# High and low parts of the transposed activations, interleaved token by token

## The chip, the cores and the metric

The kernel runs on one core of a Trainium2 chip. The metric is the device time of one execution in microseconds. All times of the profile come from one profiled execution, counted from the start of its span.

## The reference

One decoder layer on 256 tokens of width 4096: an RMS norm, one wide projection, two token mixers (chunked gated linear attention, GLA, and sliding-window attention with sinks, SWA), a gated merge, an output projection, a residual and a final norm.

```python
h = rms_norm(x, norm_gains[l])
z = h @ w_in[l]                       # 4096 -> 19472 columns
(gq, gk, gv, gg, gdec, sq, sk, sv, sg, ga, gb) = split_columns(z, IN_SPLITS)
...
o_a = gla_mix(gq, gk, gv, log_a)      # per-head norm and a SiLU gate follow
y_a = (o_a * silu(gg)) @ w_gla_out[l]
o_b = swa_sink_mix(sq, sk, sv, sinks[l])
y_b = (o_b * silu(sg)) @ w_swa_out[l]
merged = sigmoid(ga + b_gates[l, 0]) * y_a + sigmoid(gb + b_gates[l, 1]) * y_b
x = x + merged @ w_out[l]
return rms_norm(x, final_norm_gain)
```

(Shapes and casts are left out.) Everything is fp32.

## The kernel before

Nearly all of the work is in `gemm` (line 125), which multiplies 256 tokens by a block of 512 weight columns. Both operands are split into a high part, a copy rounded to the type F32R, and a low part, the difference. A product is then the sum of three matmuls, which lines 136 to 138 issue for each k tile of 128 rows and each of the two token tiles of 128: high times high, high times low, low times high. In them the activations are the stationary operand (the weights of the array, in TensorE's sense: 128 x 128, taken by a weight load before each matmul), and the weight matrix of the layer is the moving one, 128 x 512. They add up in one PSUM tile `acc` for each token tile.

The weight matrices stream from memory two k tiles at a time (`raw`, line 148, on SP's queue). ScalarE makes their high part (line 154), VectorE their low part (line 155), into staging tiles of three buffers. The scheduler orders by data and by priority; the loads and splits are raised by `tc.high_priority`.

The activations lie transposed in SBUF, 128 values of the k dimension on the partitions and tokens along the row. There are four such tiles: `hT` (the input times its gain, 32 k tiles; its first contents are made in `first_inputs` by ScalarE on line 107 and VectorE on line 108 during the first block, gq 0), `oaT` and `obT` (the outputs of the two mixers, 16 k tiles each) and `mT` (the merged output, 32 k tiles, in the place of `hT`). The last three are written by `transpose_split` (line 177): TensorE transposes into PSUM (line 184), and `split_to` makes the high part on ScalarE (line 174) and the low part on VectorE (line 175), two k tiles at a time. Of `mT`, seven of the eight groups are issued together, in the last step of the merge loop, and the eighth in the first block of the output projection.

In each of these tiles the layout is [partition, k tile, high or low, token], so that a weight load on lines 136 to 138 reads 128 neighbouring values.

Besides `gemm`, one more place reads `hT`: the low-rank input of the decays (line 215) uses it as the moving operand, 512 columns of both parts, with 32 columns of weights, into the PSUM tile `dps`; lines 219 and 220 add the two halves of the result into `gd`.

The order of the stages is: gq 0, gk 0, the decays, then for two groups of heads gq, gk, gv, gg with the GLA mixer in between; sk, sv; the eight blocks of the GLA output projection (`ya`); sq and sg four times with the SWA mixer; then ga, gb and the SWA output projection (`yb`) eight times; and the eight blocks of the output projection (`o`).

Of the kernel before, what the change touches and what calls it, by code (L numbers as in the profile page):

```python
# [8 lines left out]
F32 = mybir.dt.float32  # L9
F32R = mybir.dt.float32r  # L10
AF = mybir.ActivationFunctionType
ALU = mybir.AluOpType
AX = mybir.AxisListType

P = 128
S = 256
# [3 lines left out]
KT = DM // P  # L20
KW = 2
GH, DK, DV = 8, 128, 256
RANK = 16
CH = 64
HQ, HKV, HD = 32, 8, 64
OKT = 2048 // P
# [4 lines left out]

# 512-column blocks of w_in, in the order in which the host lays them out.
BLOCKS = []
# [13 lines left out]
def trunk_kernel(  # L47
# [18 lines left out]
    nc = tc.nc  # L66
# [20 lines left out]
    def rms_scale(o, ssum, n):  # L87
        """o = (ssum / n + eps) ** -0.5"""
        nc.vector.tensor_scalar(o, ssum, 1.0 / n, EPS, ALU.mult, ALU.add)
        nc.gpsimd.tensor_tensor(o, o, mhalf[:, : o.shape[1]], ALU.pow)  # L90

# [1 line left out]
    hT = big.tile([P, KT, 2, S], F32R, tag="hT", name="hT")  # L93

    xsb = big.tile([P, KT, S], F32, tag="oT", name="xsb")

    def first_inputs(gp, ssq):
        """Loads the input as the first block needs it; its squares add up in ssq."""

        def before(k0, n):  # L100
            with tc.high_priority(PRIO):
                if k0 < 4 or k0 % 4 == 0:
                    m = n if k0 < 4 else 4
                    nc.sync.dma_start(xsb[:, k0 : k0 + m, :], xT[:, k0 : k0 + m, :])
                for kt in range(k0, k0 + n):
                    g = gin_sb[:, kt : kt + 1]
                    nc.scalar.activation(hT[:, kt, 0, :], xsb[:, kt, :], AF.Copy, scale=g)
                    nc.vector.scalar_tensor_tensor(
                        hT[:, kt, 1, :], xsb[:, kt, :], g, hT[:, kt, 0, :].bitcast(F32), ALU.mult, ALU.subtract
                    )  # L110
            xr = xsb[:, k0 : k0 + n, :]
            if k0 < KW:
                nc.scalar.activation(ssq[:, k0 : k0 + n, :], xr, AF.Square)
                return
            sq = gp.tile([P, KW, S], F32, tag="sq", name=f"sq{k0}", bufs=2)
            nc.scalar.activation(sq, xr, AF.Square)
            nc.gpsimd.tensor_tensor(ssq, ssq, sq, ALU.add)

        return before
# [5 lines left out]
    def gemm(name, lhs, w, nkt, before=None, chunks=WHOLE, trail=0, hold=None):  # L125
        """Both token tiles of lhs.T @ w for one block of 512 columns. The second tile's products
        with the last `trail` chunks come after all of the first tile's; those of these chunks
        that the staging area can't keep until then are in `hold`."""
        acc = [acc_ps.tile([P, NB], F32, tag="acc", name=f"{name}_a{t}") for t in range(NT)]

        def products(t, k0, n, hi, lo):
            ts = slice(t * P, (t + 1) * P)
            for i in range(n):
                kt = k0 + i
                lh, ll = lhs[:, kt, 0, ts], lhs[:, kt, 1, ts]
                nc.tensor.matmul(acc[t], lh, hi[:, i, :], start=kt == 0, stop=False)  # L136
                nc.tensor.matmul(acc[t], lh, lo[:, i, :], start=False, stop=False)  # L137
                nc.tensor.matmul(acc[t], ll, hi[:, i, :], start=False, stop=kt == nkt - 1)  # L138

        chunks = [c for c in chunks if c[0] < nkt]  # L140
        held = []
        for ci, (k0, n) in enumerate(chunks):
            left = len(chunks) - ci
            if before is not None:
                before(k0, n)
            with tc.high_priority(PRIO):
                raw = stage.tile([P, n, NB], F32, tag="raw", name=f"{name}_r{k0}", bufs=4)
                nc.sync.dma_start(raw, w[k0 // KW][:, k0 % KW : k0 % KW + n, :])
                if STG < left <= trail:
                    hi, lo = hold[:, trail - left, 0], hold[:, trail - left, 1]  # L150
                else:
                    hi = stage.tile([P, n, NB], F32R, tag="hi", name=f"{name}_h{k0}")
                    lo = stage.tile([P, n, NB], F32R, tag="lo", name=f"{name}_l{k0}")
                nc.scalar.copy(hi, raw)  # L154
                nc.vector.tensor_tensor(lo, raw, hi.bitcast(F32), ALU.subtract)  # L155
            products(0, k0, n, hi, lo)
            if left <= trail:
                held.append((k0, n, hi, lo))
            else:
                products(1, k0, n, hi, lo)  # L160
        for h in held:
            products(1, *h)
        return acc
# [7 lines left out]
    def split_to(dst, src_ps):  # L171
        """dst[:, ..hi/lo.., :] from a PSUM tile of the same layout less the hi/lo axis."""
        hi, lo = dst
        nc.scalar.copy(hi, src_ps)
        nc.vector.tensor_tensor(lo, src_ps, hi.bitcast(F32), ALU.subtract)

    def transpose_split(oT, kt0, src, nk, name):
        """src [tokens, t, nk*128] -> oT[:, kt0:kt0+nk, hi/lo, tokens]"""
        for k2 in range(0, nk, 2):
            tp = pst(f"{name}_t{k2}")  # L180
            for k in range(2):
                for t in range(NT):
                    c = (k2 + k) * P
                    nc.tensor.transpose(
                        tp[:, k * S + t * P : k * S + (t + 1) * P], src[:, t, c : c + P], ident
                    )
            v = tp.rearrange("p (k s) -> p k s", k=2)
            ks = slice(kt0 + k2, kt0 + k2 + 2)
            split_to((oT[:, ks, 0, :], oT[:, ks, 1, :]), v)

    # ================= gated linear attention =================
    with tc.tile_pool(name="gla", bufs=1) as gp:
        ssq = gp.tile([P, KW, S], F32, name="ssq")
        q0 = zblock("gq", 0, before=first_inputs(gp, ssq), chunks=RAMP)
        k0 = zblock("gk", 0)
        oaT = big.tile([P, OKT, 2, S], F32R, tag="oT", name="oaT")

        # per-token scale of the input norm
        xps = pst("xps")
# [6 lines left out]

        # low-rank decay input, transposed: rows 0-15 from w's high part, 16-31 from its low part
        wd_raw = stage.tile([P, KT, RANK], F32, tag="raw", name="wd_raw", bufs=4)
# [5 lines left out]
        for kt in range(KT):  # L214
            nc.tensor.matmul(
                dps[0 : 2 * RANK, :], wd[:, kt], hT[:, kt], start=kt == 0, stop=kt == KT - 1
            )
        gd = gp.tile([2 * RANK, S], F32, name="gd")
        nc.scalar.copy(gd, dps[0 : 2 * RANK, 0:S])
        nc.vector.tensor_tensor(gd, gd, dps[0 : 2 * RANK, S : 2 * S], ALU.add)  # L220
        rps = pst("rps")
# [17 lines left out]
        def headsT(name, acc, scale):  # L239
            """[tokens, 4 heads x 128] in PSUM -> [128, head, token]"""  # L240
            zt = gp.tile([P, NT, NB], F32, tag="zt", name=f"{name}_z")
# [19 lines left out]
        for g in range(2):  # L261
            accq = q0 if g == 0 else zblock("gq", g)
            qT = headsT(f"gq{g}", accq, DK**-0.5)

            # log decays of the group's heads and their running sums in each chunk
            l = gp.tile([P, 4, S], F32, tag="e0", name=f"l{g}")
# [49 lines left out]
            nc.vector.tensor_tensor(kT, kT, d, ALU.mult)  # L316
            # keys of chunks 0 and 1 as chunks 2 and 3 see them
            k2 = gp.tile([P, 4, 2 * CH], F32, tag="k2", name=f"k2{g}")
# [7 lines left out]
            for p in range(2):  # L326
# [5 lines left out]

                # o = A @ v, a head at a time; A is kept transposed, [key, query]
                accg = None
# [55 lines left out]

    # ================= sliding-window attention =================
    late = ctx.enter_context(tc.tile_pool(name="late", bufs=1))
    ya = late.tile([P, NT, DM], F32, tag="ya", name="ya")
    with tc.tile_pool(name="swa", bufs=1) as sp:
# [37 lines left out]

        obT = big.tile([P, OKT, 2, S], F32R, tag="oT", name="obT")
        for i in range(4):
# [62 lines left out]

    # ================= gates and merge =================
    def merged(n):
        transpose_split(mT, n * 4, ya[:, :, n * NB : (n + 1) * NB], 4, f"m{n}")  # L500

    with tc.tile_pool(name="mrg", bufs=1) as mp:
        for n in range(NBLK):
# [11 lines left out]
            if n == NBLK - 1:  # L515
                mT = big.tile([P, KT, 2, S], F32R, tag="hT", name="mT")
                for m in range(n):
                    merged(m)
# [6 lines left out]

    # ================= output projection, residual, final norm =================
    with tc.tile_pool(name="fin", bufs=1) as fp:
# [38 lines left out]
def _tiles(w, nblk):  # L566
    """[K, nblk*512] -> [block, K group, partition, k tile, 512], contiguous for each load."""
    import numpy as np

    k = w.shape[0]  # L570
    w = w.reshape(k // (KW * P), KW, P, nblk, NB)
    return np.ascontiguousarray(w.transpose(3, 0, 2, 1, 4))
# [55 lines left out]
```

## Time and profile before

| | us |
|---|---|
| median of 3 runs (lowest to highest) | 2496.63 (2496.22 to 2498.13) |
| span of the profiled execution | 2494.7 |
| TensorE busy (PE) | 2469.9 (99%) |
| weight loads busy (PEld) | 2033.3 (82%) |
| VectorE busy (DVE) | 1306.1 (52%) |
| ScalarE busy (ACT) | 1093.1 (44%) |
| GpSimd busy (POOL) | 41.4 (2%) |

The profile counts TensorE's matmuls (PE) and its weight loads (PEld) as two engines. Matmuls are pipelined and their ends are modelled, so a matmul's shown time is longer than the step from one start to the next; the starts are what tells the pace. The time of the profiled execution is its span, 2494.7 us; the time of a run holds some 2 us more.

### The profile page before, as it was taken

How to read it: one execution, taken by the hardware profiler on the slowest of the kernel's cores; microseconds unless marked ns; L12 is line 12 of the kernel's file. 1: busy time of each engine (PE TensorE's matmuls, PEld its weight loads, DVE VectorE, ACT ScalarE, POOL GpSimd, SP SyncE). 2: the span in 40 equal slices, each digit the busy share in tenths (PEclk: the TensorE clock that was granted, in tenths of full speed). 3: DMA queues.
4: the chain of work that ended last, by engine and by line, in shares of the span. 5: the costliest groups of instructions: out<-in, count | busy, mean ns of one | idle time of the engine just before them, and what ended most of it. 6: DMA issues, size and time to landing. Idle time of an engine off the chain costs nothing.

```text
span 2494.7 us, 28744 instructions
## 1 busy us (share of the span) xinstructions
PE 2469.9 (99%) x11220; PEld 2033.3 (82%) x11220; DVE 1306.1 (52%) x1303; ACT 1093.1 (44%) x1289; POOL 41.4 (2%) x52
## 2 busy tenths in 40 slices
PE   8999999999999999999999999999999999999998
PEld 6788888888888888888888888888888888888886
DVE  8565555545444455555555454555545456544544
ACT  6444444434444444544444444444444444444443
POOL 4000000000000000000000000000000000000000
PEclk9999999999999999999999999999999999999999
DMA  7455555445555545454465556665666555665655
GB/s 258 156 175 188 170 175 195 175 168 188 194 192 195 193 148 193 150 171 166 150 211 199 198 198 197 197 202 197 198 196 198 194 194 177 236 211 203 211 203 186
DMA packets 132985, 474.32 MB, mean 190 GB/s; under 512 B 15056, under 2 KB 15440, under 8 KB 132720
## 3 DMA queue, kind: packets, MB, share of 16 engines
q1 hardware_dynamic: 127584, 461.69, 54.5%
q10 hardware_dynamic: 5264, 10.79, 1.4%
q8 instruction: 88, 1.44, 0.2%
q14 instruction: 49, 0.40, 0.0%
HBM read 468.23 MB, written 4.19 MB: 189 GB/s over the span
## 4 chain that ended last, share of the span: by engine, by line
PE 95%; DVE 2%; issue 1%; ACT 1%; DMA 0%; POOL 0%; SPq 0%; ACTq 0%; POOLq 0%; DVEq 0%
PE ga_a L137 5%; PE ga_a L136 5%; PE gb_a L137 5%; PE gb_a L136 5%; PE ga_a L138 5%; PE gb_a L138 5%; PE o_a L136 5%; PE o_a L137 5%; PE o_a L138 5%; PE sg_a L137 2%; PE sg_a L136 2%; PE sg_a L138 2%; PE sq_a L138 2%; PE sq_a L137 2%; PE ya_a L136 2%; PE ya_a L137 2%
## 5 line engine op out<-in xcount | busy, mean ns | idle before, releaser
L155 DVE TENSOR_TENSOR ga_l<-ga_r,ga_h 128x1024 fp32r<-128x1024 f32 x128 | 156.8, 1225 | 171.6 <-ACT ga_h L154 171.6
L155 DVE TENSOR_TENSOR gb_l<-gb_r,gb_h 128x1024 fp32r<-128x1024 f32 x128 | 156.9, 1225 | 171.1 <-ACT gb_h L154 171.1
L155 DVE TENSOR_TENSOR o_l<-o_r,o_h 128x1024 fp32r<-128x1024 f32 x124 | 152.0, 1225 | 161.4 <-ACT o_h L154 161.3
L154 ACT CAST ga_h<-ga_r 128x1024 fp32r<-128x1024 f32 x128 | 135.2, 1057 | 209.8 <-PE ga_a L138 171.5
L154 ACT CAST gb_h<-gb_r 128x1024 fp32r<-128x1024 f32 x128 | 135.2, 1056 | 204.5 <-PE gb_a L138 159.4
L154 ACT CAST o_h<-o_r 128x1024 fp32r<-128x1024 f32 x124 | 131.0, 1056 | 193.2 <-PE o_a L138 186.2
L138 PE MATMUL ga_a<-ga_h,hT 128*128 128x512 f32 x512 | 199.4, 389 | 0.0
L137 PE MATMUL ga_a<-ga_l,hT 128*128 128x512 f32 x512 | 199.2, 389 | 0.0
L136 PE MATMUL ga_a<-ga_h,hT 128*128 128x512 f32 x512 | 199.2, 389 | 0.0
L138 PE MATMUL gb_a<-gb_h,hT 128*128 128x512 f32 x512 | 199.2, 389 | 0.0
L136 PE MATMUL gb_a<-gb_h,hT 128*128 128x512 f32 x512 | 199.2, 389 | 0.0
L137 PE MATMUL gb_a<-gb_l,hT 128*128 128x512 f32 x512 | 199.2, 389 | 0.0
L138 PE MATMUL o_a<-o_h,mT 128*128 128x512 f32 x496 | 193.0, 389 | 0.0
L137 PE MATMUL o_a<-o_l,mT 128*128 128x512 f32 x496 | 193.0, 389 | 0.0
L136 PE MATMUL o_a<-o_h,mT 128*128 128x512 f32 x496 | 192.9, 389 | 0.0
L155 DVE TENSOR_TENSOR ya_l<-ya_r,ya_h 128x1024 fp32r<-128x1024 f32 x64 | 78.4, 1226 | 95.6 <-ACT ya_h L154 95.6
L155 DVE TENSOR_TENSOR sq_l<-sq_r,sq_h 128x1024 fp32r<-128x1024 f32 x64 | 78.4, 1225 | 84.8 <-ACT sq_h L154 84.8
L155 DVE TENSOR_TENSOR yb_l<-yb_r,yb_h 128x1024 fp32r<-128x1024 f32 x64 | 78.4, 1225 | 82.8 <-ACT yb_h L154 82.8
L155 DVE TENSOR_TENSOR gg_l<-gg_r,gg_h 128x1024 fp32r<-128x1024 f32 x64 | 78.3, 1224 | 75.9 <-ACT gg_h L154 75.9
L155 DVE TENSOR_TENSOR sg_l<-sg_r,sg_h 128x1024 fp32r<-128x1024 f32 x64 | 78.3, 1223 | 72.7 <-ACT sg_h L154 72.7
L154 ACT CAST sg_h<-sg_r 128x1024 fp32r<-128x1024 f32 x64 | 67.4, 1053 | 111.0 <-PE sg_a L138 94.7
L155 DVE TENSOR_TENSOR gv_l<-gv_r,gv_h 128x1024 fp32r<-128x1024 f32 x64 | 78.2, 1224 | 67.9 <-ACT gv_h L154 67.9
(278 smaller groups left out, 5568.3 us busy)
## 6 DMA issues: line engine op xcount, KB each, us to landing
ga_r<-in_win_dram SPq DMA_DIRECT2D x128, 512.0 KB, 4.3
gb_r<-in_win_dram SPq DMA_DIRECT2D x128, 512.0 KB, 4.2
o_r<-in_wout_dram SPq DMA_DIRECT2D x128, 512.0 KB, 3.3
gv_r<-in_win_dram SPq DMA_DIRECT2D x64, 512.0 KB, 3.2
gg_r<-in_win_dram SPq DMA_DIRECT2D x64, 512.0 KB, 3.3
ya_r<-in_wgla_dram SPq DMA_DIRECT2D x64, 512.0 KB, 3.2
sq_r<-in_win_dram SPq DMA_DIRECT2D x64, 512.0 KB, 3.2
sg_r<-in_win_dram SPq DMA_DIRECT2D x64, 512.0 KB, 3.3
```

The costliest lines, as they stand in the source:

```text
L136: nc.tensor.matmul(acc[t], lh, hi[:, i, :], start=kt == 0, stop=False)
L137: nc.tensor.matmul(acc[t], lh, lo[:, i, :], start=False, stop=False)
L138: nc.tensor.matmul(acc[t], ll, hi[:, i, :], start=False, stop=kt == nkt - 1)
L154: nc.scalar.copy(hi, raw)
L155: nc.vector.tensor_tensor(lo, raw, hi.bitcast(F32), ALU.subtract)
```

## The change

In `hT`, `oaT`, `obT` and `mT` the two innermost axes change places: the layout becomes [partition, k tile, token, high or low]. The high and the low value of a token are neighbours, and a weight load reads 128 values with one value between each two. All writers and readers of these tiles follow. For the decays, the moving operand is still the same 512 neighbouring values, and the two halves of the result, which now alternate too, are picked out of PSUM with a step. (The diff also takes out comments and docstrings, which is not shown.)

```diff
-    hT = big.tile([P, KT, 2, S], F32R, tag="hT", name="hT")
+    hT = big.tile([P, KT, S, 2], F32R, tag="hT", name="hT")
...
-                    nc.scalar.activation(hT[:, kt, 0, :], xsb[:, kt, :], AF.Copy, scale=g)
+                    nc.scalar.activation(hT[:, kt, :, 0], xsb[:, kt, :], AF.Copy, scale=g)
                     nc.vector.scalar_tensor_tensor(
-                        hT[:, kt, 1, :], xsb[:, kt, :], g, hT[:, kt, 0, :].bitcast(F32), ALU.mult, ALU.subtract
+                        hT[:, kt, :, 1], xsb[:, kt, :], g, hT[:, kt, :, 0].bitcast(F32), ALU.mult, ALU.subtract
                     )
...
-                lh, ll = lhs[:, kt, 0, ts], lhs[:, kt, 1, ts]
+                lh, ll = lhs[:, kt, ts, 0], lhs[:, kt, ts, 1]
...
-            split_to((oT[:, ks, 0, :], oT[:, ks, 1, :]), v)
+            split_to((oT[:, ks, :, 0], oT[:, ks, :, 1]), v)
...
-        oaT = big.tile([P, OKT, 2, S], F32R, tag="oT", name="oaT")
+        oaT = big.tile([P, OKT, S, 2], F32R, tag="oT", name="oaT")
...
-                dps[0 : 2 * RANK, :], wd[:, kt], hT[:, kt], start=kt == 0, stop=kt == KT - 1
+                dps[0 : 2 * RANK, :], wd[:, kt], hT[:, kt].rearrange("p s h -> p (s h)"), start=kt == 0, stop=kt == KT - 1
...
-        nc.scalar.copy(gd, dps[0 : 2 * RANK, 0:S])
-        nc.vector.tensor_tensor(gd, gd, dps[0 : 2 * RANK, S : 2 * S], ALU.add)
+        d2 = dps[0 : 2 * RANK, :].rearrange("p (s h) -> p h s", h=2)
+        nc.scalar.copy(gd, d2[:, 0, :])
+        nc.vector.tensor_tensor(gd, gd, d2[:, 1, :], ALU.add)
...
-        obT = big.tile([P, OKT, 2, S], F32R, tag="oT", name="obT")
+        obT = big.tile([P, OKT, S, 2], F32R, tag="oT", name="obT")
...
-                mT = big.tile([P, KT, 2, S], F32R, tag="hT", name="mT")
+                mT = big.tile([P, KT, S, 2], F32R, tag="hT", name="mT")
```

## Rows read from the trace of the kernel before

**Rows 1.** The page: busy us (share) and instructions by engine; granted clock by slice.

```profile
PE 2469.9 (99%) x11220; PEld 2033.3 (82%) x11220; DVE 1306.1 (52%) x1303; ACT 1093.1 (44%) x1289; POOL 41.4 (2%) x52
...
PEclk9999999999999999999999999999999999999999
```

**Rows 2.** The page: the chain that ended last, by engine.

```profile
PE 95%; DVE 2%; issue 1%; ACT 1%; DMA 0%; POOL 0%; SPq 0%; ACTq 0%; POOLq 0%; DVEq 0%
```

**Rows 3.** The timeline (start us, us, engine, line) inside a ga block.

```profile
1500.19 0.39 PE L137 MATMUL ga_a<-ga_l,hT 128*128 128x512 f32 x1
1500.20 0.19 PEld L138 LDWEIGHTS ga_a<-ga_h,hT 128*128 128x128 f32 x1
1500.42 0.39 PE L138 MATMUL ga_a<-ga_h,hT 128*128 128x512 f32 x1
...
1503.82 0.39 PE L138 MATMUL ga_a<-ga_h,hT 128*128 128x512 f32 x1
```

**Rows 4.** Weight loads by shape: count | busy us, mean ns | idle before.

```profile
L138 PEld LDWEIGHTS ga_a<-ga_h,hT 128*128 128x128 f32 x512 | 96.1, 188 | 19.9
...
L215 PEld LDWEIGHTS dps<-hT,wd 128*32 128x32 f32 x32 | 3.4, 109 | 3.7
L345 PEld LDWEIGHTS at<-qs,ks 128*64 128x64 f32 x32 | 3.1, 134 | 0.0
```

**Rows 5.** Tile dps: duration ns min/median/max, first and last start us.

```profile
L215 PE MATMUL dps<-hT,wd x32: 387/392/400, 102.9 to 110.0; 128*32 128x512 f32 x32
```

**Rows 6.** Timeline in the SWA mixer: loads of 128 columns for matmuls of 64.

```profile
910.27 0.30 PEld L481 LDWEIGHTS so<-sv,pT 128*128 128x128 f32 x2 [0.21 <-ACT pT L480]
...
910.49 0.30 PEld L482 LDWEIGHTS so<-sv,pT 128*128 128x128 f32 x2
```

**Rows 7.** Timeline in the first block, after a wait of TensorE for data.

```profile
26.27 0.19 PEld L137 LDWEIGHTS gq_a<-gq_l,hT 128*128 128x128 f32 x1 [0.32 <-DVE gq_l L155]
26.27 0.50 PE L137 MATMUL gq_a<-gq_l,hT 128*128 128x512 f32 x1
...
26.38 0.19 PEld L138 LDWEIGHTS gq_a<-gq_h,hT 128*128 128x128 f32 x1
26.61 0.40 PE L138 MATMUL gq_a<-gq_h,hT 128*128 128x512 f32 x1
```

**Rows 8.** VectorE's groups by shape: a copy with a step, one without.

```profile
L308 DVE COPY dec<-e 128x16 f32<-128x16 f32 x2 | 0.3, 170 | 0.0
...
L224 DVE COPY rb<-rstd 128x32 f32<-128x32 f32 x2 | 0.3, 178 | 0.8 <-POOL rstd L90 0.8
```

**Rows 9.** TensorE's matmuls by shape: the slowest and an undisturbed group.

```profile
L137 PE MATMUL ga_a<-ga_l,hT 128*128 128x512 f32 x512 | 199.2, 389 | 0.0
...
L137 PE MATMUL gq_a<-gq_l,hT 128*128 128x512 f32 x128 | 51.4, 402 | 5.2 <-DVE gq_l L155 5.2
```

**Rows 10.** First 60 us: busy of PE, PEld, DVE, ACT, POOL; low halves; first matmul.

```profile
0.00:60.00 60.00, 49.07 (x199) 37.80 (x200) 49.44 (x52) 42.61 (x71) 26.22 (x25) 1.00 0.75 262
...
L108 DVE SCALAR_TENSOR_TENSOR hT<-xsb,gin_sb,hT 128x256 fp32r<-128x256 f32 x32 | 27.1, 897 | 4.4 <-ACT hT L107 4.4
...
3.81 0.48 DVE L108 SCALAR_TENSOR_TENSOR hT<-xsb,gin_sb,hT 128x256 fp32r<-128x256 f32 x1 [3.81 <-ACT hT L107]
...
5.39 0.80 PE L136 MATMUL gq_a<-gq_h,hT 128*128 128x512 f32 x1 [5.39 <-ACT gq_h L154]
```

**Rows 11.** The splits by shape, VectorE's and ScalarE's.

```profile
L155 DVE TENSOR_TENSOR ga_l<-ga_r,ga_h 128x1024 fp32r<-128x1024 f32 x128 | 156.8, 1225 | 171.6 <-ACT ga_h L154 171.6
...
L175 DVE TENSOR_TENSOR mT<-m_t,mT 128x512 fp32r<-128x512 f32 x16 | 9.9, 682 | 0.3 <-ACT mT L174 0.3
...
L154 ACT CAST ya_h<-ya_r 128x1024 fp32r<-128x1024 f32 x64 | 67.6, 1057 | 95.3 <-PE ya_a L138 91.3 <-PE sv_a L138 4.0
...
L174 ACT CAST mT<-m_t 128x512 fp32r<-128x512 f32 x16 | 8.7, 591 | 0.3
```

**Rows 12.** Busy by engine around the transposes of mT.

```profile
2100.00:2130.00 30.00, 29.96 (x161) 25.31 (x160) 20.47 (x25) 17.16 (x25) 0.00 (x0) 1.00 0.43 150
```

## The prediction

> **What bounds the kernel now.** I read the shares of the engines first, then the chain that ended last, then a few microseconds of the timeline in the middle of a projection, and last the groups of weight loads by shape. TensorE is busy for 2469.9 us of the span of 2494.7 us and the chain of work is 95% TensorE [rows 1, 2]. The weight loads, counted as an engine of their own (PEld), are busy 82% of the span, VectorE 52%, ScalarE 44% [rows 1]. [...]
>
> In the stream the matmuls of lines 136 to 138 start at an even step: from 1500.19 to 1503.82 us there are 16 steps, 3.63 / 16 = 0.227 us each [rows 3]. There are 38 blocks of w_in with 32 k tiles, 16 blocks of the two branch projections with 16, and 8 of w_out with 32, each k tile with 3 products for 2 token tiles: (38 x 32 + 16 x 16 + 8 x 32) x 6 = 10,368 matmuls. Times 0.227 us that is 2354 us, 94% of the span. So the question is what the change does to this step of 0.227 us, and all else is small.
>
> **What sets the step.** Each weight load starts when the matmul before its own has started, and is shown for 0.19 us; 0.22 to 0.23 us after its start its own matmul starts [rows 3]. This leaves open whether the matmul or the load sets the pace. Three rows decide. First, the 32 matmuls into dps also have 512 columns but load only 32 columns of weights, shown for 109 ns in place of 188 [rows 4], and still start every (110.0 - 102.9) / 31 = 0.229 us [rows 5]. A load shorter by 79 ns bought nothing. Second, the shown time of a load isn't the time for which it holds up the next. It is 109, 134 and 188 ns for 32, 64 and 128 columns, so 79 / 96 = 0.82 ns a column, 105 ns for 128, over a fixed part of some 83 ns [rows 4]. Where a matmul is only 64 columns wide, two loads of 189 ns each fit into 0.30 us, and the pairs follow one another every 0.22 us: a new load every 0.11 us [rows 6]. The fixed part of one overlaps with the next. Third, where TensorE had waited for data, the load starts at 26.27, the next load at 26.38 and the next matmul at 26.61 us [rows 7]: the weights were in after 0.11 us, and the matmul then took its 0.23 us. So of every step of 0.227 us the load needs about 0.11, and about 0.12 us is slack.
>
> **The change, part by part.** No instruction is added or removed. Three kinds of access get a step of two fp32 values (8 bytes): the weight reads of the 10,368 matmuls, the writes of the two halves (and VectorE's read of the high half), and two reads from PSUM.
>
> *Weight reads.* No row of before shows TensorE reading with a step. The bounds: at one end the column keeps its 0.82 ns and the step costs nothing. At the other, taking every second value costs as much as passing over the value between, twice 0.105 to 0.11 = 0.21 to 0.22 us. The only read with a step in this trace is VectorE's copy into dec, 16 values 64 apart: 170 ns, against 178 ns for a copy of 32 values without that step [rows 8]. So even at a step of 256 bytes a value costs no more than two. In the stream both ends are under 0.227 us: zero at the lower end, zero at the upper end with 0.01 us to spare. Cover would be gone where a load isn't started under a full matmul: after a wait, or after a row of transposes. Such matmuls are shown for 0.50 instead of 0.39 us [rows 7]. I count them from the groups of matmuls: gq_a of line 137 has a mean of 402 ns over 128, the undisturbed ga_a 389 ns [rows 9]; the excess over 389 ns, summed over the 39 groups of lines 136 to 138 (those two rows are the largest and the undisturbed), is about 14 us, or at most some 140 matmuls of 0.1 us. At twice the load each would lose 0.11 us more: 0 to +16 us. I take 0, because at 8 bytes the nearest row has a step 32 times as wide and stays below twice.
>
> [...]
>
> *Writes.* In the first block ScalarE writes 32 high halves and VectorE 32 low halves (897 ns on average, 0.48 us when undisturbed) [rows 10]. VectorE is busy 49.4 of the first 60 us and TensorE only 49.1, so here VectorE's time counts [rows 10]. Bounds: nothing, or two slots for every value. From 512 to 1024 columns VectorE needs 1225 - 682 = 543 ns more [rows 11], or 272 ns for 256; 32 x 0.272 = +8.7 us. ScalarE needs (1057 - 591) / 2 = 233 ns more per 256 [rows 11], 7.5 us in all, but it is busy only 42.6 of 60 us [rows 10], so this hides. Later halves come from transposes: 16 pairs for mT and 8 each for oaT and obT. The tightest place is the 14 pairs for mT issued together near 2106 us. There VectorE is busy 20.5 of 30 us [rows 12], and doubling would add 14 x 0.543 = 7.6 us into 9.5 us of idle time. I take 0 for it and for the first block, again by the copy into dec [rows 8]; ends 0 and +16 us, if that idle time didn't cover.
>
> *PSUM reads.* gd is built by a copy on ScalarE and an addition on VectorE, of 256 values each, in front of the decays. Twice the slots would be, by the same 233 and 272 ns [rows 11], 0.5 us at most. I take 0.
>
> *Order.* The halves of one k tile now share one stretch of addresses. If waits are drawn by stretches, line 136 would also wait for the low half of its k tile, in the first block only. There line 137 waits anyway for gq_l, which comes from the same VectorE queue after that half; the whole idle time of TensorE in the first 60 us is 10.9 us, and 5.4 of it is the start [rows 10]. I price it at 0 to 2 us and take 0.
>
> The sum: 2494.7 + 0 as a span. The median of the three runs is 2496.63 us, 1.9 us more than the span shown; I forecast 2497 us.
>
> **The rivals.**
> *The shown time of the load is what counts (slower).* If a load has to be over, as shown, before its matmul starts, the slack is only 0.227 - 0.188 = 0.039 us, and a load of twice 0.105 us streaming plus 0.083 us takes 0.293 us. The step becomes 0.293, and 10,368 x 0.066 = 684 us come on top: 3180 us. It decides from a load of 1.4 times the columns' time on. For it: 82% of busy loads [rows 1]. Against it: loads that start 0.11 us apart while each is shown for 0.19 [rows 6]. A load that streams for more than 0.227 us, over 2.1 times as long, would end alike; nothing in the trace points to so much. Chance 0.11.
>
> [...]
>
> *The load doubles and the stream hides it, but the 140 switches don't.* +16 us: 2513 us. Against it: the copy into dec. Chance 0.06.
>
> *Writes with a step cost double.* The first block grows by 8.7 us, in the worst case 16 us with the mT halves: 2505 to 2513 us. Chance 0.07.
>
> *It does less than it says, or helps.* A new order of the first block could save some of TensorE's 5.5 us of waits after its start, for 2491 us; the dps rows exclude a gain in the step itself, since even a load of 32 columns leaves it at 0.229. Chance 0.05.
>
> **How the numbers follow.** No change, 2497 us, has the remaining 0.71. I call within 0.2% (5 us) the same, about what a measurement of this kernel can tell from no change. Faster: 0.05. Slower: 0.11 + 0.06 + 0.07 = 0.24. The range goes from 2490 to 2514 us: it takes in both costs of some 16 us and the small gain, and leaves out only the first rival.
>
> **What would show it.** In the trace of after: the step in the middle of a projection, 0.227 us if I am right, about 0.29 if the first rival is. The shown weight load of ga_a: 188 ns if the step is free, about 293 ns if a column takes twice as long. In that case a stream still at 0.227 us confirms the slack and refutes that price alone. VectorE's low halves in the first block at some 900 ns and those of mT at 682 ns if writes are free, 272 and 543 ns more if not. The end of the first block then tells what it cost. I would be wrong if the load's own time rose past 0.227 us, or if the fixed part can't overlap behind a long matmul as it does behind a short one.

## The result and the profile after

The changed kernel takes 2569.96 us (median of 3 runs, 2569.42 to 2570.79) against 2496.63 us: a ratio of 1.0293, 95% interval 1.0275 to 1.0311. It is slower by 73 us, where 2497 us, between 2490 and 2514, had been forecast.

The page of after, the engines' busy times, as in [rows 1]:

```profile
span 2568.2 us, 28744 instructions
...
PE 2546.0 (99%) x11220; PEld 2108.5 (82%) x11220; DVE 1304.2 (51%) x1303; ACT 1090.5 (42%) x1289; POOL 42.2 (2%) x52
```

The instructions are the same 28744. TensorE is busy 76.1 us longer and idle 2.6 us less (2568.2 - 2546.0 = 22.2, before 24.8), together the 73.5 us by which the span has grown. VectorE and ScalarE have not grown. So the time is in the matmuls themselves. The timeline inside a ya block and an o block (start us, us, engine, line), to be read against [rows 3]:

```profile
699.65 0.40 PE L136 MATMUL ya_a<-ya_h,oaT 128*128 128x512 f32 x1
...
703.89 0.40 PE L136 MATMUL ya_a<-ya_h,oaT 128*128 128x512 f32 x1
...
2299.75 0.39 PE L136 MATMUL o_a<-o_h,mT 128*128 128x512 f32 x1
...
2301.85 0.39 PE L136 MATMUL o_a<-o_h,mT 128*128 128x512 f32 x1
```

In ya there are 18 steps in 4.24 us, 0.2356 us each; in o 9 steps in 2.10 us, 0.2333 us each. Before, it was 0.2267 in both kinds of block. The groups of weight loads by shape (count, busy us, mean ns, idle) show the same two kinds of block:

```profile
L138 PEld LDWEIGHTS ga_a<-ga_h,hT 128*128 128x128 f32 x512 | 101.2, 198 | 19.1
...
L137 PEld LDWEIGHTS o_a<-o_l,mT 128*128 128x128 f32 x496 | 95.8, 193 | 19.8
```

A load is shown for 193 to 195 ns in one kind (gk, gv, gg, sk, sq, sg, o, and gq but for its slow start) and 196 to 198 in the other (sv, ya, ga, gb, yb), against 188 in [rows 4]. By count, with 0.2356 - 0.2267 us more in the second kind and 0.2333 - 0.2267 in the first, that is 4800 x 8.9 ns + 5568 x 6.6 ns = 80 us, about what TensorE has grown. A load grew by 5 to 10 ns and had some 120 ns of cover, and still every matmul is 7 to 9 ns late.

VectorE's strided writes, answering [rows 10, 11]:

```profile
L108 DVE SCALAR_TENSOR_TENSOR hT<-xsb,gin_sb,hT 128x256 fp32r<-128x256 f32 x32 | 22.0, 735 | 3.8 <-ACT hT L107 3.8
...
L175 DVE TENSOR_TENSOR mT<-m_t,mT 128x512 fp32r<-128x512 f32 x16 | 9.9, 684 | 0.3 <-ACT mT L174 0.3
```

VectorE's writes cost nothing (684 ns for 682, and in the first block 735 for 897). ScalarE's high halves of mT went from 591 to 646 ns, 55 ns on 16 instructions, hidden. The copy and the addition of gd from PSUM take 361 and 409 ns, before 362 and 409. In the first 60 us TensorE is busy 50.9 us, not less than the 49.1 of before.

### The profile page after: what moved, and what is told of

The parts are those of the page before. It is cut to its first block, busy times and chain, and to the rows that moved or that the text cites. A ratio compares the mean times of both kernels' runs of the same rounds, so it can differ in the third digit from the quotient of the medians.

```text
span 2568.2 us, 28744 instructions
## 1 busy us (share of the span) xinstructions
PE 2546.0 (99%) x11220; PEld 2108.5 (82%) x11220; DVE 1304.2 (51%) x1303; ACT 1090.5 (42%) x1289; POOL 42.2 (2%) x52
## 4 chain that ended last, share of the span: by engine, by line
PE 98%; issue 1%; DVE 1%; ACT 0%; POOL 0%; DMA 0%; SPq 0%; ACTq 0%; POOLq 0%; DVEq 0%
PE gb_a L138 5%; PE ga_a L138 5%; PE gb_a L137 5%; PE gb_a L136 5%; PE ga_a L137 5%; PE ga_a L136 5%; PE o_a L136 5%; PE o_a L138 5%; PE o_a L137 5%; PE sg_a L137 2%; PE ya_a L137 2%; PE yb_a L138 2%; PE ya_a L136 2%; PE ya_a L138 2%; PE yb_a L137 2%; PE yb_a L136 2%
## 5 line engine op out<-in xcount | busy, mean ns | idle before, releaser
L138 PE MATMUL ga_a<-ga_h,hT 128*128 128x512 f32 x512 | 204.4, 399 | 0.0
L138 PE MATMUL gb_a<-gb_h,hT 128*128 128x512 f32 x512 | 204.3, 399 | 0.0
L136 PE MATMUL gb_a<-gb_h,hT 128*128 128x512 f32 x512 | 202.8, 396 | 0.0
L136 PE MATMUL ga_a<-ga_h,hT 128*128 128x512 f32 x512 | 202.7, 396 | 0.0
L137 PEld LDWEIGHTS gb_a<-gb_l,hT 128*128 128x128 f32 x512 | 100.4, 196 | 21.7
L137 PEld LDWEIGHTS ga_a<-ga_l,hT 128*128 128x128 f32 x512 | 100.3, 196 | 21.7
L138 PEld LDWEIGHTS gb_a<-gb_h,hT 128*128 128x128 f32 x512 | 101.2, 198 | 19.1
```

## The experiments

### Which half of the change: reads or writes

The first kernel keeps the layout of before and makes the weight loads read every second token; the second has the layout of the change and reads neighbours.

```diff
-                lh, ll = lhs[:, kt, 0, ts], lhs[:, kt, 1, ts]
+                lh, ll = (lhs[:, kt, q, :].rearrange("p (s b) -> p s b", b=2)[:, :, t] for q in range(2))
```

> The layout of before, but the weight loads of lines 136 to 138 take every second of the 256 tokens of a part (token tile 0 the even ones, tile 1 the odd ones), so that reads have the step of the change and writes have none. Rows of the result are permuted, which the mixers do not undo. Theory 1 (the step of the reads alone makes the matmul step longer): about 2570 us, the step in a projection 0.233 to 0.235 us. Theory 2 (the written layout, its order or its addresses do it): about 2497 us, 0.227 us.

```diff
-                lh, ll = lhs[:, kt, ts, 0], lhs[:, kt, ts, 1]
+                lh, ll = (lhs[:, kt].rearrange("p s h -> p (s h)")[:, (2 * t + q) * P : (2 * t + q + 1) * P] for q in range(2))
```

> The layout of the change with all its writes, but the weight loads take 128 neighbouring values (64 tokens, high and low mixed), so that the products are of other values than the reference's. Theory 1: about 2497 us, step 0.227 us. Theory 2: about 2570 us. If both halves of the change cost, this and the run before each show a part of the 73 us.

Measured: reads with a step and no other change 2567.14 us, ratio 1.0273 [1.0255, 1.0291], with one run of four at 2558.3 us and the others at 2567 to 2568; the interleaved layout with neighbouring reads 2497.98 us, ratio 1.0003 [0.9993, 1.0013]. The timelines in one ya block of the first and one ga block of the second kernel:

```profile
700.13 0.39 PE L136 MATMUL ya_a<-ya_h,oaT 128*128 128x512 f32 x1
...
703.63 0.39 PE L136 MATMUL ya_a<-ya_h,oaT 128*128 128x512 f32 x1
```

```profile
1699.65 0.39 PE L136 MATMUL ga_a<-ga_h,hT 128*128 128x512 f32 x1
...
1703.73 0.39 PE L136 MATMUL ga_a<-ga_h,hT 128*128 128x512 f32 x1
```

3.50 / 15 = 0.2333 us with the step in the reads, 4.08 / 18 = 0.2267 us without. Theory 1 holds: the reads alone carry the loss, the whole of it as far as the intervals can tell. The writes, the PSUM reads and any new order of the first block, all that the second kernel has of the change, cost nothing that can be measured.

### Matmuls alone, by the step of the weight read

This kernel runs rows of 96 equal matmuls, weights from one tile and moving columns from another, with nothing beside them.

```python
nc.tensor.matmul(acc[0:cols, 0:n], weights(step, cols, i), moving(1, n, i), ...)
# weights: 128 values at the given step from place (i % 4) * 1024; moving: n neighbours from (i % 4) * 1024
```

> Not the layer: 16 rows of 96 matmuls in F32R and nothing beside them, each with one step of the weight read (1, 2, 3, 4, 8) and 512, 256 or 64 moving columns. Theory 1a (a longer load delays its matmul only when it is longer than the matmul under which it runs): with 512 columns all steps give 0.227 us, with 64 columns the start-to-start time of the loads tells the load's own time, 0.11 us at step 1 and more at step 2. [...]

The timeline of TensorE, one line for a row of matmuls (name: step of the weights, then a for 512, c for 256 moving columns; "mvtwotwo" has step 2 in both operands; oned and onehalf only end the row before them). From one line's start to the next line's, divided by the count, is the step from matmul to matmul. The row of step 1 with 512 columns came first, and its first eleven matmuls took 0.43 us each or more; the figure for step 1, 0.2267 us, is from rows of the next kernel of this kind, (40.05 - 29.17) / 48:

```profile
40.03 22.56 PE L68 MATMUL twoa<-mv,wt 128*128 128x512 f32 x96
62.43 22.77 PE L68 MATMUL threea<-mv,wt 128*128 128x512 f32 x96
85.03 22.73 PE L68 MATMUL foura<-mv,wt 128*128 128x512 f32 x96
107.60 23.71 PE L68 MATMUL eighta<-mv,wt 128*128 128x512 f32 x96
131.14 43.68 PE L68 MATMUL mvtwotwo<-mv,wt 128*128 128x512 f32 x96
174.64 22.27 PE L68 MATMUL onehalf<-mv,wt 128*64 128x512 f32 x96
...
262.27 11.70 PE L68 MATMUL onec<-mv,wt 128*128 128x256 f32 x96
273.80 11.68 PE L68 MATMUL twoc<-mv,wt 128*128 128x256 f32 x96
285.32 15.91 PE L68 MATMUL oned<-mv,wt 128*128 128x64 f32 x96
```

Step 2 gives 22.40 / 96 = 0.2333 us, the kernel's own figure, with no other engine at work beside the matmuls but to copy out each row's result: the loss needs nothing but TensorE's matmuls and their weight loads. Step 3 gives 0.2354, step 4 0.2351, step 8 0.2452 us. With 256 moving columns steps 1 and 2 take the same 0.120 us. So theory 1a falls (step 2 costs at 512 columns). The cost does not grow in proportion to the step (6.6, 8.7, 8.4 and 18.5 ns at steps 2, 3, 4 and 8), and at 256 columns there is none. With 64 columns of weights (rows half shown) step 1 itself takes 0.2303 and step 2 0.2316 us, 1.3 ns more. The rows with 64 moving columns ran in part at the lower clock (granted 0.50 to 0.66) and are not used; the next kernel repeats them.

### One load in three

```diff
-                lh, ll = lhs[:, kt, 0, ts], lhs[:, kt, 1, ts]
+                lh, ll = lhs[:, kt, 0, ts], lhs[:, kt, 1, :].rearrange("p (s b) -> p s b", b=2)[:, :, t]
```

> The layout of before; only the loads of line 138 (the low part, one load in three) take every second token, so token tile 0 meets the even tokens' low parts. Theory A (a load with a step slows the matmul under which it runs): the step from line 137 to line 138, under which that load runs, becomes 0.233 us, the two others stay 0.227; 3456 x 6.7 ns = +23 us, 2520 us. Theory B (it slows the matmul that uses it): the step from line 138 to line 136 becomes 0.233, the same +23 us. Theory C (one read with a step upsets the even cadence of all three): all three steps longer, +50 us or more.

Measured: 2537.74 us, ratio 1.0165 [1.0148, 1.0182], +41 us. The timeline in a yb block:

```profile
1700.10 0.39 PE L136 MATMUL yb_a<-yb_h,obT 128*128 128x512 f32 x1
1700.33 0.39 PE L137 MATMUL yb_a<-yb_l,obT 128*128 128x512 f32 x1
1700.56 0.40 PE L138 MATMUL yb_a<-yb_h,obT 128*128 128x512 f32 x1
1700.79 0.39 PE L136 MATMUL yb_a<-yb_h,obT 128*128 128x512 f32 x1
...
1703.57 0.39 PE L136 MATMUL yb_a<-yb_h,obT 128*128 128x512 f32 x1
```

All three steps are about 0.23 us (3.47 / 15 = 0.2313); over the whole run their means are 0.2301 to 0.2324. One load with a step out of three lengthens also the two matmuls whose loads have none. That is theory C, a little cheaper than the 50 us expected. The step is not a price for each load that can be added up.

### Step four in the kernel

```diff
-                lh, ll = lhs[:, kt, 0, ts], lhs[:, kt, 1, ts]
+                lh, ll = (lhs[:, kt].rearrange("p h (s b) -> p (h s) b", b=4)[:, :, 2 * t + q] for q in range(2))
```

> The layout of before; the loads take every fourth of the 512 values of a k tile, high and low parts mixed, so that the products are of other values. From the rows of matmuls alone (0.2333 us at step 2, 0.2350 at step 4, before 0.2267): 2497 + 10,368 x 8.3 ns = about 2583 us. [...]

Measured: 2591.8 us, ratio 1.0382 [1.0361, 1.0402], near the 2583 us from the rows alone. Loads and starts in an o block:

```profile
L137 PEld LDWEIGHTS o_a<-o_l,mT 128*128 128x128 f32 x496 | 153.6, 310 | 0.0
```

```profile
2299.74 0.39 PE L136 MATMUL o_a<-o_h,mT 128*128 128x512 f32 x1
...
2303.97 0.40 PE L136 MATMUL o_a<-o_h,mT 128*128 128x512 f32 x1
```

A load is shown for 310 ns, yet matmuls start every 4.23 / 18 = 0.2350 us. So the shown time of a load does not bound the step, as the prediction argued against its first rival; and the step of four costs only 1.7 ns more here than the step of two does. The ga, gb and yb blocks ran at 0.2367 us, which is most of what lies between 2583 and 2591.8. Whether the load's own time, without the part that overlaps with the next, now sets the pace is taken up in the next section.

### The load's own time, and what address and length do

> Not the layer: 32 rows of 20 to 48 matmuls in F32R with other steps, offsets of the weights, weight columns and moving columns, and nothing beside them. Theory A (the read with a step competes with the running matmul's own read): alternating loads of step 1 and 2 give 0.227 and 0.233 us in turn; with 448, 384 and 320 moving columns step 2 costs 5 to 7 ns more than step 1 too, until the matmul is as short as the load itself (0.12 us, as at 256 columns, where both took 0.120). The load's own time in the rows of 64 moving columns between full ones, at the upper clock: 0.11 us at steps 1 to 3. Rival (the load with a step itself takes up to 0.23 us and is no longer hidden): 0.2 us or more in the rows of 64 columns at step 2, and 0.233 us with 448, 384 and 320 moving columns alike. If the addresses decide (both reads meeting in the same part of the memory), rows with the weights moved by 1, 4, 16 or 128 values differ from 0.233 us.

Rows as above. "Narrow" rows have 64 moving columns and follow a row of full ones, so that the load sets the pace (a matmul of 64 columns would take 0.2267 / 8 = 0.028 us, an estimate from the rows of 512); the granted clock of the narrow rows is 1.00 (of filld, which only ends the last of them, 0.81). "fill" rows are the full ones between; "cols..." have 32 columns of weights; "contoffsixteen" reads neighbouring weights, 16 values later:

```profile
118.20 11.36 PE L82 MATMUL contoffsixteen<-mv,wt 128*128 128x512 f32 x48
129.40 11.36 PE L82 MATMUL contoffrow<-mv,wt 128*128 128x512 f32 x48
...
212.94 11.28 PE L82 MATMUL colsthirtytwoone<-mv,wt 128*32 128x512 f32 x48
224.05 11.36 PE L82 MATMUL colsthirtytwotwo<-mv,wt 128*32 128x512 f32 x48
235.25 2.31 PE L82 MATMUL narrowone<-mv,wt 128*128 128x64 f32 x20
237.40 7.55 PE L82 MATMUL filla<-mv,wt 128*128 128x512 f32 x32
244.78 2.43 PE L82 MATMUL narrowtwo<-mv,wt 128*128 128x64 f32 x20
247.05 7.54 PE L82 MATMUL fillb<-mv,wt 128*128 128x512 f32 x32
...
265.14 4.63 PE L82 MATMUL narrowfour<-mv,wt 128*128 128x64 f32 x20
269.60 9.14 PE L82 MATMUL filld<-mv,wt 128*128 128x512 f32 x32
```

Narrow: the load's own time is 2.15 / 20 = 0.108 us at step 1, 2.27 / 20 = 0.114 at step 2, 4.46 / 20 = 0.223 at step 4. The gap between the first two matmuls of each row is only 0.03 us; without it the steps are 0.112, 0.118 and 0.233 us. The rival (a load of up to 0.23 us that is no longer hidden) is out: at step 2 the load is 6 ns longer. At step 4 it isn't out: there the load's own 0.233 us is more than the 0.2267 us of the matmul over it, so in the kernel with step four, at 0.2350 us, the load itself may set the pace. So at step 2 the load's own time was not the problem.

Theory A is also wounded. In rows not shown, step 2 costs nothing with 384 moving columns (0.173 us, 0.174 at step 1), and one load in four with a step (0.2317 us) costs more than every second one (0.2302, which is what theory A gives on average). The row that turned the study is contoffsixteen: weights that are neighbours, no step at all, only 64 bytes further on, and 11.20 / 48 = 0.2333 us, the full price of the change. And a load of only 32 columns, in order, makes 0.2315 us: a shorter load, a longer step.

### Only addresses

> Not the layer: 32 rows of 42 matmuls (128 columns of weights, 512 moving columns) with the addresses of the weights and of the moving operand moved against each other. Theory E (what counts is when the two reads meet, which the addresses set; a step only spoils the meeting): neighbouring weights moved by 1 to 64 values give 0.230 to 0.235 us, moved by 128, 256 or 512 values (whole 512 bytes) 0.227; step 2 gives 0.233 us wherever it starts, since it runs through twice the addresses. Moving both by 16 tells whether the difference or the place itself counts. [...]

Here w and m name which operand starts later, and the number is by how many values (4 bytes each). No row shown has a step but fixedtwo and fixedtwowsixteen, whose matmuls all read one and the same place, where those of the other rows go through two or three; twobases only ends the row before it:

```profile
75.99 9.96 PE L85 MATMUL wsixteen<-mv,wt 128*128 128x512 f32 x42
85.79 9.93 PE L85 MATMUL wthirtytwo<-mv,wt 128*128 128x512 f32 x42
95.55 9.69 PE L85 MATMUL wsixtyfour<-mv,wt 128*128 128x512 f32 x42
105.09 9.68 PE L85 MATMUL wrow<-mv,wt 128*128 128x512 f32 x42
114.61 9.68 PE L85 MATMUL wtworows<-mv,wt 128*128 128x512 f32 x42
...
152.90 9.78 PE L85 MATMUL msixteen<-mv,wt 128*128 128x512 f32 x42
162.51 9.71 PE L85 MATMUL msixtyfour<-mv,wt 128*128 128x512 f32 x42
...
181.57 9.72 PE L85 MATMUL bothsixteen<-mv,wt 128*128 128x512 f32 x42
191.13 9.70 PE L85 MATMUL basec<-mv,wt 128*128 128x512 f32 x42
...
219.99 10.05 PE L85 MATMUL fixedtwo<-mv,wt 128*128 128x512 f32 x42
229.88 9.82 PE L85 MATMUL fixedtwowsixteen<-mv,wt 128*128 128x512 f32 x42
239.54 9.71 PE L85 MATMUL twobases<-mv,wt 128*128 128x512 f32 x42
```

Weights 16 values later: 0.2333 us; 32 values: 0.2324; 64 values (256 bytes): 9.54 / 42 = 0.2271; 128 values: 9.52 / 42 = 0.2267, and the same for 256 and 512. Weights 1 to 8 values later, in rows not shown, take 0.2307 to 0.2333 us. The moving operand 16 values later: 0.2288; both 16 later: 0.2276, and 0.226 over the last 28 matmuls of that row, from 184.79 us on. So it is the difference that counts, in whole 256 bytes. At step 2 it is 0.2333 us wherever the weights start in the rows that go through three places; in the rows that read one place it is 9.89 / 42 = 0.2355 us, and with the weights 16 values later 9.66 / 42 = 0.2300. So the loss needs no step; theory E holds, but for the 256 in place of 512 bytes and for these two rows: the address counts at step 2 too.

### The same in the kernel, without any step

The first version let all four tiles start 64 bytes later, each made 64 bytes longer.

```diff
-    hT = big.tile([P, KT, 2, S], F32R, tag="hT", name="hT")
+    hT = big.tile([P, KT * 2 * S + OFF], F32R, tag="hT", name="hT")[:, OFF:].rearrange("p (k h s) -> p k h s", h=2, s=S)
...
```

> The layout of before, neighbouring reads, all values right; only the four tiles of activations start 16 values (64 bytes) later in their place. Theory E: the step of the matmuls becomes 0.233 us, 10,368 x 6.7 ns = +69 us, 2566 us, although no read has a step. [...]

Measured: 2513.07 us, ratio 1.0066 [1.0049, 1.0083]: slower, but by 16 us. The shift was not the one intended. Two tiles, each longer by 64 bytes, lie ahead of the staging tiles, which so moved by 128 bytes: against them hT lies 64 bytes earlier, not later, and oaT and obT have kept their place. The timeline where a yb block ends and a ga block begins:

```profile
1700.33 0.39 PE L137 MATMUL yb_a<-yb_h,obT 128*128 128x512 f32 x1
...
1702.37 0.39 PE L137 MATMUL ga_a<-ga_h,hT 128*128 128x512 f32 x1
...
1703.75 0.39 PE L137 MATMUL ga_a<-ga_h,hT 128*128 128x512 f32 x1
```

2.04 / 9 = 0.2267 us in yb, and 1.38 / 6 = 0.230 us in ga (0.2289 as the mean of the ga blocks), near the row with the moving operand 16 values later (0.2288). (Lines are moved by one in this kernel.) That the places follow the order in which tiles are made was argued here; the next pair tested it by moving hT and mT alone:

```diff
+    def shifted(name):
+        t = big.tile([P, KT * 2 * S + 64], F32R, tag="hT", name=name)
+        return t[:, OFF : OFF + KT * 2 * S].rearrange("p (k h s) -> p k h s", h=2, s=S)
...
-    hT = big.tile([P, KT, 2, S], F32R, tag="hT", name="hT")
+    hT = shifted("hT")
...
-                mT = big.tile([P, KT, 2, S], F32R, tag="hT", name="mT")
+                mT = shifted("mT")
```

With OFF = 16:

> The layout of before, neighbouring reads, all values right; hT and mT alone get 64 values more room, and their contents start 16 values (64 bytes) into it, so that all other tiles move by 256 bytes together and oaT and obT keep their place against the staging tiles. Theory E (the weights' addresses against the moving operand's, in 256 bytes, set how the two reads meet): by the row of matmuls with the weights 16 values later, 0.2333 us in the blocks that read hT and mT, 7296 + 1536 = 8832 matmuls x 6.7 ns = +59 us, 2556 us; the ya and yb blocks stay at 0.2267. Theory F (only a step costs): 2497 us.

With OFF = 64:

> As the run with hT and mT shifted by 16 values, but by 64 values (256 bytes). Theory E: 2497 us, 0.2267 us everywhere. If any shift of the two tiles costs (a neighbour moved, another order of the instructions): as slow as the shift by 16.

Measured: by 64 bytes 2548.36 us, ratio 1.0207 [1.0190, 1.0224]; by 256 bytes 2496.28 us, ratio 0.9999 [0.9990, 1.0009]. The kernel shifted by 64 bytes, in a ya block (oaT, not shifted) and a gb block (hT, shifted), with lines moved by five:

```profile
700.10 0.39 PE L142 MATMUL ya_a<-ya_l,oaT 128*128 128x512 f32 x1
...
702.82 0.39 PE L142 MATMUL ya_a<-ya_l,oaT 128*128 128x512 f32 x1
```

```profile
1699.90 0.39 PE L142 MATMUL gb_a<-gb_l,hT 128*128 128x512 f32 x1
...
1702.00 0.40 PE L142 MATMUL gb_a<-gb_l,hT 128*128 128x512 f32 x1
```

2.72 / 12 = 0.2267 us and 2.10 / 9 = 0.2333 us in one and the same run. The 52 us are a little less than the 59 forecast. Nothing reads with a step here, the loads are shown for their old 188 ns, and the matmul step is that of the changed kernel. It is theory E, inside the kernel.

How far hT moved against the staging tiles follows from the order of the tiles, if it is as argued above. The 64 values of room move the staging tiles by 256 bytes in both kernels. With OFF = 64, hT moves with them and keeps its place: this run shows that the room and a move of everything cost nothing, and that 256 bytes of difference cost nothing is shown by the rows of matmuls alone. With OFF = 16, hT lies 256 - 64 = 192 bytes earlier against them, which modulo 256 is 64 bytes later, and 0.2333 us is the step of the row with the weights 16 values later; 64 bytes earlier, in the kernel with all four tiles shifted, gave 0.2289.

## Why the prediction was wrong

*What bounds the kernel* was right: the step of the matmul stream decides, and the change came in through it.

*The load's own time* was right: at most twice, nearer to nothing; it is 0.114 for 0.108 us (0.118 for 0.112 without each row's first gap). Where it was expected to end, at 188 ns shown against 293, it ended at 193 to 198.

*The step that failed* is in the part on the weight reads: "In the stream both ends are under 0.227 us: zero at the lower end, zero at the upper end with 0.01 us to spare." It took a load under the cover of a matmul for free as long as it is shorter than the matmul. The runs showed in its place that the step depends on where the load and the running matmul read. How the two addresses lie to each other, and how they advance, changed it: 0.2267 us where they agree modulo 256 bytes and both read neighbours, 0.229 to 0.2333 us where neighbours start 64 bytes off, and with a step of two 0.2333 to 0.2356 us in the kernels, 0.2300 to 0.2355 in the rows at 512 columns. That the loss at a step of two and the loss at 64 bytes are one and the same interaction is argued from these figures, not shown. The kernel before had the shortest step of all that were tried with 512 columns, and its code doesn't ask for it: its weights start at multiples of 512 bytes within their tiles.

*The sign that was misread* stands in [rows 5]. The dps matmuls, with a load of 32 columns, step by 0.229 us; I read this as "a load shorter by 79 ns bought nothing". The starts there are rounded to 0.1 us, so that 0.229 can't be told from 0.227; read to 0.01 us, from the first matmul at 102.86 to the 28th at 109.07 us, the step is 6.21 / 27 = 0.230. It is longer than 0.227, and the row of 32 columns without other work agrees (0.2315). The dps weights also start at steps of 128 bytes, so the addresses may have their part in it. A shorter read that makes the step longer was the mark of an interaction, and no row of before excluded one.

*The first rival* (the shown time counts, 3180 us) had the right sign and a wrong mechanism: at step 4 loads shown for 310 ns still leave a step of 0.235 us. The loads' busy share, which spoke for it, is 82% before and after, so it doesn't show the loss, and of each step of 0.2267 us the load itself needs 0.112, about half. At step 4, where the loads of o, ga and gb (310 to 316 ns) have no idle time before them, the load's own 0.233 us may bound the step.

*Writes, PSUM reads, order* were right at zero: 2497.98 us for the whole layout without the strided reads. *The switches* cost nothing that had to be looked for. *The range* left out the one case that came, because the interaction was not among the cases; for 73 us, between a forecast of 0 and a rival of 684, the prediction had no mechanism.

## What to carry to other kernels

A weight load that is hidden under a matmul is hidden in time only: a load of neighbours needs 0.108 us of its own, and with weights that start 64 bytes later the step still went from 0.2267 to 0.2333 us. In a stream of 512-column matmuls in F32R, read the weights as neighbours and let their start and the moving operand's agree modulo 256 bytes (0.2267 and 0.2271 us in the rows); moving the contents of two tiles by 64 bytes cost 2% here with no other mark in the trace than a step of 0.233 in place of 0.227 us. Measure the step from start to start over many matmuls, to the nanosecond, for it is this number, times 10,368 here, that is the kernel's time.

## What the runs showed of the hardware that was not expected

- The step depends on the difference of the two addresses (rows at 0.2267, 0.2271, 0.2288, 0.2324, 0.2333 us), and the cost of a step of two is gone at 384 (0.173 us, 0.174 at step 1) and 256 moving columns (0.120 us at both). Weights that start 64 bytes later, with nothing else changed, make every matmul 6.7 ns longer (0.2333 us for 0.2267). What lies behind it was not tried and stays open.
- A step in the moving operand is another matter: with the moving columns at step 2 a matmul takes (174.64 - 131.14) / 96 = 0.453 us, twice as long (0.451 with the weights at step 1).
- The changed kernel has two even rhythms, 0.2333 and 0.2356 us, each kept through one or many whole blocks. The first sq block, which follows the ya blocks without a break, ran at 0.236 us (905.29 to 908.83 us, 3.54 / 15) and the second, after the SWA mixer, at 0.2333 us (974.81 to 976.91 us, 2.10 / 9), both from hT. So the tile that is read doesn't alone choose; what does is open. The rows that read one place at step 2 gave 0.2355 and 0.2300 us, so the addresses have a part in it.
